# A hybrid decoder layer on one core: the fourth unit's delta net inputs ahead of the third unit's q and k projections, with two more homes for two buffers

## The chip, the core and the metric

The kernel runs on one core of one Trainium2 chip. The core has five engines with queues of their own: PE (TensorE, matmuls), DVE (VectorE), ACT (ScalarE), POOL (GpSimd) and SP (SyncE, which here only issues DMAs; ACT issues some too). [...] The metric is the device time of one execution in microseconds (us).

## The reference

One layer on 2048 tokens of width 1024, all float32. A first norm and one input projection feed three mixers side by side; their outputs are joined, projected, added to x, and a SwiGLU network follows:

```python
h = rms_norm(x, norm1_g)
u_conv, u_qkv, u_z, u_ab, u_dq, u_dk, u_dv = split(h @ w_in)
y_conv = conformer_conv_mixer(u_conv, ...)          # 31 taps, layer norm, silu
y_gdn  = gated_deltanet_mixer(u_qkv, u_z, u_ab, ...)  # 4 heads of 64, chunks of 64 tokens
y_diff = differential_attention_mixer(u_dq, u_dk, u_dv, ...)
x = x + concat([y_conv, y_gdn, y_diff]) @ w_out
gate, up = split(rms_norm(x, norm2_g) @ w_ffn_in)
x = x + (silu(gate) * up) @ w_ffn_out
return rms_norm(x, final_norm_g)
```

The delta net works by chunks of 64 tokens. For each chunk a lower triangular matrix (here L) is built from k, the gates g and beta; its inverse (here X64) is applied; then a scan carries a 64x64 state per head from chunk to chunk:

```python
lower = where(strict, beta * (k @ k.T) * decay, 0)
sol   = triangular_solve(lower + eye, [v * beta, k * beta * exp(g)])
def step(state, inp):                  # 32 chunks, one after the other
    v_new = u_i - w_i @ state
    o_i   = (q_i * exp(g_i)) @ state + qk_i @ v_new
    state = state * exp(g_last) + (k_i * exp(g_last - g_i)).T @ v_new
```

## The kernel before

The 2048 tokens are four units of 512 (u = 0 to 3), each of four token tiles of 128. Products that need float32 accuracy are three matmuls of split operands (mm3, lines 137 to 139). The program text makes the mixers' part of the kernel as a list of steps, each a letter and a unit (line 937):

- N: ln1, the first norm of a unit; eight groups of four transposes (tiles ntp, line 292) that ACT and DVE write as the two halves of h (tiles ht, lines 302 and 303).
- I: gdn_in, inputs of the delta net: z and the gates (PSUM tiles mz, one per token tile), then q, k, v in six tiles (mq) with their short convolution (gdn_conv), and between them gdn_decays, which makes L and QKT.
- G: gdn_unit: k k^T and q k^T (tiles kk), products into L and QKT; the 32x32 inverses on DVE in 31 steps (tm, Tt, lines 470 and 472), out to DRAM and back as the merged inverse X64 (tile X in the trace), whose last block needs yp and wp; then the scan over eight chunks (tiles vp, op, dp, state Sbd).
- C and L: the convolution mixer: projections mg and mv and 62 tap instructions on DVE (tiles cp, ca); then its layer norm (tiles ctp, ctq).
- K and V: q, k projections (eight tiles ma, each with a second half ql on DVE) and v projections (mw), stored to DRAM.
- A: attention of the first unit (tiles s, pt, po, to).

After the list come the first half of unit 0's output projection (tiles hp, fed by hx), and the rest: attention of units 1 to 3 mixed with output projection (po from line 137) and the SwiGLU network (pg, pu, pd) of unit after unit.

The framework writes every engine's queue when the program is built, by readiness on its own estimate and by priority: an instruction's place in the text, moved ahead where the text says hp(n). So the list of steps is an order of preference and no barrier. What is strict are the buffers. A tile belongs to a tag with a number of slots. Tags that matter here: wp (split weights, 3 slots, every weight piece of the kernel takes the next one); wraw (raw weights before their split, 2 slots of 1024 numbers per partition; the split of w_in is kept in DRAM after unit 0, so units 1 to 3 load wp directly and take no raw slot); mm0 and mm1 (two PSUM banks, in turn for every tile mz, mq, mg, mv, ma, mw and unit 3's ctp, ctq); tp (2 PSUM banks for ntp, kt1, gtp and others); L, dd and tg (one slot each in pool gd: L; the decays' tg and the merge's ys share dd; the decays' bm and the inverses' tm share tg); X64 is one constant tile for all units. Pools gd and ps_sc (two PSUM banks of the scan) end after hp, and the output projection's tiles take their place.

Of the kernel before, what the change touches and what calls it, by code (L numbers as in the profile page):

```python
# [10 lines left out]
F32 = mybir.dt.float32  # L11
# [7 lines left out]
P = 128  # L19
# [5 lines left out]
TU = U // P  # L25
IN_W = 3080
H = 4
C = 64
DFF = 2816
NF = DFF // P  # L30
WS = 1024
# [11 lines left out]
def bcast(ap, n):  # L43
    return ap.unsqueeze(len(ap.shape)).to_broadcast(list(ap.shape) + [n])
# [3 lines left out]
def body(ctx: ExitStack, tc: tile.TileContext, x, norm1_g, w_in, conv_dw_w, conv_dw_b,  # L48
# [3 lines left out]
    V, G, A, T = nc.vector, nc.gpsimd, nc.scalar, nc.tensor  # L52
# [20 lines left out]
    def cst(shape, name):  # L73
        return const.tile(shape, F32, name=name, tag=name)
# [23 lines left out]
    wpool = ctx.enter_context(tc.tile_pool(name="wpool", bufs=1))  # L98
    wcount = [0]

    def hp(n=4000):
        return tc.high_priority(offset=n)
# [57 lines left out]
    def bank(*b):  # L160
        return Rot([P, 512], F32, *b)
# [14 lines left out]
    gd = gctx.enter_context(tc.tile_pool(name="gd", bufs=1, side="right"))  # L176
# [34 lines left out]
    nc.sync.dma_start(stg[33:34, 0:256], conv_ln_b)  # L211
    stq = gd.tile([4, 768], F32, name="stq", tag="L")
    nc.sync.dma_start(stq, gdn_conv_w[0])
# [31 lines left out]
    V.memset(ones, 1.0)  # L245
    Sbd = cst([P, 2, P], "Sbd")
    V.memset(Sbd, 0.0)
    X64 = cst([P, H, TU, C], "X64")
    V.memset(X64, 0.0)
    hist4 = cst([P, 6, 3], "hist4")  # L250
    V.memset(hist4, 0.0)
    hist30 = cst([P, 2, 30], "hist30")
# [127 lines left out]

    def gdn_decays(u, sc):

        L = sc["L"] = gd.tile([P, H, TU, C], F32, name=f"L{u}", tag="L")
        QKT = sc["QKT"] = gd.tile([P, H, TU, C], F32, name=f"Q{u}", tag="QKT", bufs=2)

        def m4(m):
            return m.unsqueeze(1).unsqueeze(1).to_broadcast([P, 2, H, C])

        for t0 in range(0, TU, 2):
            t2 = slice(t0, t0 + 2)  # L390
            tg = gd.tile([P, 2, H, C], F32, name=f"tg{u}_{t0}", tag="dd")
            V.tensor_tensor(tg, m4(mT), bcast(sc["g"][:, t2, :], C), op=ALU.mult)
            gr = ps_ga.tile([P, 512], F32, name=f"gr{u}_{t0}", tag="ga")
            T.matmul(gr, lhsT=bones, rhs=tg.rearrange("p t h c -> p (t h c)"), start=True, stop=True)
            bm = gd.tile([P, 2, H, C], F32, name=f"bm{u}_{t0}", tag="tg")
            G.tensor_tensor(bm, m4(mN), bcast(sc["be"][:, t2, :], C), op=ALU.mult)
            Lt, Qt = (d_[:, :, t2, :].rearrange("p h t c -> p t h c") for d_ in (L, QKT))
            V.tensor_tensor(Qt, gr.rearrange("p (t h c) -> p t h c", t=2, h=H), bcast(sc["G"][:, t2, :], C),
                            op=ALU.subtract)
            V.tensor_tensor(Lt, Qt, m4(mN), op=ALU.mult)  # L400
            V.tensor_tensor(Qt, Qt, m4(mT), op=ALU.mult)
            A.activation(Lt, Lt, AF.Exp, scale=-1.0)
            A.activation(Qt, Qt, AF.Exp)
            G.tensor_tensor(Qt, Qt, m4(mT), op=ALU.mult)
            V.tensor_tensor(Lt, Lt, bm, op=ALU.mult)
# [22 lines left out]
        sc.update(c1=c1, c2=c2, c3=c3)  # L428

    def gdn_unit(u, qtok, sc):  # L430
        L, QKT = sc["L"], sc["QKT"]

        def qkh(tt):
            return qtok[:, tt, 0:512].rearrange("p (h d) -> p h d", d=C)
        for tt in range(TU):
# [10 lines left out]
            for hp in range(2):  # L446
                kk = ps_ga.tile([P, 512], F32, name=f"kk{u}_{tt}_{hp}", tag="ga")
                kv = kk[:, 0:256].rearrange("p (a b c) -> p a b c", a=2, b=2)
                for p in range(2):
                    for ch in range(2):  # L450
# [3 lines left out]
                                 skip_group_check=True)  # L454
                for d_, b in ((L, 0), (QKT, 1)):
                    V.tensor_tensor(d_[:, hp::2, tt, :], kv[:, :, b, :], d_[:, hp::2, tt, :], op=ALU.mult)
        nc.scalar.dma_start(gL[u].rearrange("h (t p) c -> p (h t) c", p=P), L.rearrange("p h t c -> p (h t) c"))

# [18 lines left out]
        for ch in range(2):  # L477
            for blk in range(2):
                r0 = ch * C + blk * 32
                nc.scalar.dma_start(  # L480
                    X64[r0:r0 + 32, :, :, blk * 32:blk * 32 + 32].rearrange("p h t c -> p (h t) c"),
                    gT[u][1, blk].rearrange("h (t c) s q -> c s (h t) q", c=2)[ch])
# [4 lines left out]
        for ch in range(2):  # L487
            r0 = ch * C
            for th in range(TU * H):
                T.matmul(yp[r0:r0 + 32, th * 32:th * 32 + 32], lhsT=L[r0 + 32:r0 + 64, th % H, th // H, 0:32],  # L490
                         rhs=X64[r0 + 32:r0 + 64, th % H, th // H, 32:64], start=th == 0, stop=th == TU * H - 1,
                         skip_group_check=True)
# [9 lines left out]
        for r0 in (0, 64):  # L502
            A.mul(X64[r0:r0 + 32, :, :, 32:64].rearrange("p h t x -> p t h x"),
                  wp[r0:r0 + 32, :].rearrange("p (t h x) -> p t h x", t=TU, h=H), -1.0)
# [13 lines left out]
        def scan_tr(tt, ch, pg_, WQ, ps):  # L518

            cs = slice(ch * C, ch * C + C)  # L520
            for h in range(H):
                T.matmul(ps[h % 2 * C:h % 2 * C + C, 256 + h // 2 * C:256 + h // 2 * C + C], lhsT=pg_[cs, 4 + h, :],
                         rhs=X64[cs, h, tt, :], start=True, stop=True, skip_group_check=True)
            T.transpose(ps[:, 384:512], pg_[:, 2 * ch:2 * ch + 2, :].rearrange("p h d -> p (h d)"), ident)
# [6 lines left out]
        for tt in range(TU):  # L531
            _, kdv, WQ, zr = nin
            op = ps_sc.tile([P, 512], F32, name=f"op{u}_{tt}", tag="o")
            for ch in range(2):
# [6 lines left out]
                for h in range(H):  # L541
                    T.matmul(vp[cs, h * C:h * C + C], lhsT=X64[cs, h, tt, :], rhs=kdv[cs, 4 + h, :],
                             start=h == 0, stop=False, skip_group_check=True)
# [15 lines left out]
                for h in range(H):  # L559
                    p, hp = h // 2, h % 2  # L560
# [89 lines left out]
    def gdn_in(u):  # L650

        hts = HT[u]
        pc = w_in_pieces(COL_Z, 264)
        abt = gd.tile([P, TU, 8], F32, name=f"abt{u}", tag="abt")
        for tt in range(TU):
            ps = mmt(f"mz{u}_{tt}")
            y_tile(ps[:, 0:264], hts, pc, tt)
            zs = gd.tile([P, 256], F32, name=f"zs{u}_{tt}", tag="zs", bufs=2)
            with hp():
                V.tensor_copy(abt[:, tt, :], ps[:, 256:264])  # L660
                A.activation(zs, ps[:, 0:256], AF.Tanh, scale=0.5)
                V.scalar_tensor_tensor(zs, zs, 1.0, ps[:, 0:256], op0=ALU.add, op1=ALU.mult)
            nc.scalar.dma_start(zd[u * U + tt * P:u * U + (tt + 1) * P, :], zs)
        with hp(6000):
            SC[u] = gdn_gates(u, abt)
        with hp(DP):
            gdn_decays(u, SC[u])
        qtok = QT[u] = gd.tile([P, TU, 768], F32, name=f"qtok{u}", tag="qtok", bufs=2)
        for ft in range(6):
            ps = mmt(f"mq{u}_{ft}")  # L670
            x_tile8(ps, hts, w_col_piece(w_in, COL_QKV + ft * P))
            with hp(CP):
                gdn_conv(u, ps, ft, qtok)
            if ft == 3:
                with hp(SP):
                    gdn_scales(u, qtok, SC[u])
# [257 lines left out]


    CV = {}
    for step in ("I0 C0 G0 V0 N1 K0 L0 I1 G1 N2 C1 L1 K1 V1 I2 G2 C2 N3 K2 I3 G3 L2 C3 V2 A0 K3 V3 L3").split():
        what, u = step[0], int(step[1])
        if what == "N":
            HT[u] = ln1(u)  # L940
        elif what == "I":
            gdn_in(u)
        elif what == "G":
            with hp(GP):
                gdn_unit(u, QT[u], SC[u])
        elif what == "K":
            attn_qk(u)
        elif what == "V":
            attn_v(u)
        elif what == "C":  # L950
            CV[u] = conv_taps(u, conv_in(u))
        elif what == "L":
            conv_ln(u, CV[u])
        else:
            p1bctx.close()
            ps0 = ctx.enter_context(tc.tile_pool(name="ps0", bufs=1, space=PSUM, reuse_waits="tile"))
            b0 = slots(ps0, "b0", 4)
            sct, ptt, tot, pot = (bank(b) for b in b0)
            E0, W0 = (p1b.tile([P, 4096], F32, name=f"arena{g}", tag=f"ht{g}") for g in range(2))
            X0, X1 = (p1b.tile([P, D], F32, name=f"arenx{g}", tag=f"x1{g}") for g in range(2))  # L960
            Ep, Wp = cut(E0, 1024, 4), cut(W0, 1024, 4)
            Eq = [e[:, 512:1024] for e in Ep]
            AT.update(e0=Views(F32, *(e[:, 0:512] for e in Ep)), dm=Views(F32, Eq[0]), ob=Views(F32, *cut(Eq[1], 256, 2)),
                      e1=Views(F32, *Eq[2:4]), on=Views(F32, *(f3(c_) for c_ in cut(X0[:, 0:512], 256, 2))),
                      vv=Views(F32R, f4(Wp[0])), kk=Views(F32R, *cut(Wp[1], 512, 2)), pp=Views(F32R, f3(Wp[2])),
                      qq=Views(F32R, *(f3(c_) for c_ in cut(Wp[3], 512, 2) + cut(X1, 512, 2))))
            so_ = [0]

            def take(w, m):
                o = so_[0]  # L970
                so_[0] += w * m
                vs_ = cut(X0[:, 512 + o:], w, m)
                return Views(F32, *([v.rearrange("p (a b) -> p a b", a=2) for v in vs_] if w == 4 else vs_))
            AT.update(small(take))
            dm = dists(U)
            run(attn_unit(0))
# [287 lines left out]
```

## Time and profile before

| | before |
|---|---|
| runs, us | 2917.52, 2921.23, 2925.54 (median 2921.23) |
| the profiled execution: time, us | 2917.14 |
| its span from first to last instruction, us | 2915.4 |
| mean granted TensorE clock | 0.982 |
| PE busy | 2800.1 us (96%) |
| DVE, ACT, POOL busy | 1565.9, 1050.0, 1111.3 us |

Times inside the profile count from the first instruction. The four units' steps up to V3 fill the span to about 834 us; the stretch from there to about 992 us is the change of stage to the SwiGLU network, which fills the rest. The clock is granted as a share of full speed, 1.0 or 0.5. A line such as "idle before <- releaser" tells how long an engine stood before an instruction and what ended the wait. A busy PE isn't PE at its peak, since matmuls overlap: the distance from one start to the next is its real pace.

### The profile page before, as it was taken

The page shows a single profiled execution, that of the slowest core. Times are in us where ns is not written, and L with a number is a line of the kernel's source. Part 1 is how long each engine was busy: PE and PEld are TensorE (multiplying, and loading weights), DVE is VectorE, ACT ScalarE, POOL GpSimd, SP SyncE. Part 2 cuts the span into 40 slices and gives each one's busy share as a digit, 9 for nine tenths or more (in the row PEclk, how much of TensorE's full clock was granted, in tenths as well). Part 3 has the DMA queues.
Part 4 walks back from the last instruction along what each step waited for, and adds up shares of the span by engine and source line. Part 5 has one row for each costly group of instructions (what it writes and reads, how often), then busy time and mean ns, then how long its engine had stood idle before and what let it go on. Part 6 is the DMA issues. An engine that isn't in the chain of part 4 may idle for free.

```text
span 2915.4 us, 39754 instructions
## 1 busy us (share of the span) xinstructions
PE 2800.1 (96%) x14673; PEld 2284.4 (78%) x14673; DVE 1565.9 (54%) x3443; ACT 1050.0 (36%) x2237; POOL 1111.3 (38%) x1021
## 2 busy tenths in 40 slices
PE   7979989999988999999998999999999999999998
PEld 6867777778776788887877888887878888888886
DVE  8976776877766765565566655541332222422223
ACT  4333223322154544444455434442332222322222
POOL 4421010001033444344455434444644444444543
PEclk9989999999988999999999999999999999999999
DMA  7784573654776544444366344324343333323332
GB/s 253 242 274 153 178 232 127 207 179 138 254 200 219 144 131 122 112 126 118 108 182 203 86 130 120 93 88 151 102 149 99 96 94 101 116 87 102 101 94 87
DMA packets 404064, 422.52 MB, mean 145 GB/s; under 512 B 46448, under 2 KB 326170, under 8 KB 392606
## 3 DMA queue, kind: packets, MB, share of 16 engines
q1 hardware_dynamic: 344222, 373.31, 41.8%
q10 hardware_dynamic: 59648, 46.67, 5.1%
q8 instruction: 116, 1.90, 0.3%
q14 instruction: 78, 0.64, 0.1%
HBM read 344.35 MB, written 75.56 MB: 144 GB/s over the span
## 4 chain that ended last, share of the span: by engine, by line
PE 80%; DVE 8%; DMA 6%; issue 2%; ACT 2%; POOL 1%; ACTq 0%; SPq 0%; POOLq 0%; DVEq 0%
PE pg L137 6%; PE pg L138 6%; PE pg L139 6%; PE pu L139 5%; PE pu L137 5%; PE pu L138 5%; PE pd L137 5%; PE pd L138 5%; PE pd L139 5%; PE s L784 3%; PE pt L830 2%; PE po L137 1%; PE po L138 1%; PE po L139 1%; PE ma L137 1%
## 5 line engine op out<-in xcount | busy, mean ns | idle before, releaser
L121 POOL TENSOR_TENSOR wp<-wr,wp 128x512 fp32r<-128x512 f32 (+1 forms) x666 | 906.7, 1386 | 865.4 <-ACT wp L120 847.9
L120 ACT CAST wp<-wr 128x512 fp32r<-128x512 f32 (+1 forms) x666 | 378.6, 617 | 871.5 <-PE pd L139 229.1
L137 PE MATMUL pd<-wp,ac 128*128 128x512 f32 x704 | 279.8, 400 | 9.2 <-DVE x L1154 7.6
L1154 DVE TENSOR_TENSOR x<-x,pd 128x512 f32<-128x512 f32 x192 | 130.4, 685 | 285.6 <-PE pd L139 285.2
L137 PE MATMUL pg<-h,wp 128*128 128x512 f32 x704 | 279.6, 397 | 3.4 <-ACT h L1075 1.7
L138 PE MATMUL pd<-wp,ac 128*128 128x512 f32 x704 | 277.1, 394 | 2.1 <-POOL wp L121 2.1
L139 PE MATMUL pd<-wp,ac 128*128 128x512 f32 x704 | 277.5, 394 | 1.5 <-DVE ac L1138 1.5
L139 PE MATMUL pu<-h,wp 128*128 128x512 f32 x704 | 278.4, 396 | 0.0
L139 PE MATMUL pg<-h,wp 128*128 128x512 f32 x704 | 278.3, 395 | 0.0
L137 PE MATMUL pu<-h,wp 128*128 128x512 f32 x704 | 277.3, 394 | 0.6 <-DVE ft L1135 0.6
L138 PE MATMUL pu<-h,wp 128*128 128x512 f32 x704 | 277.8, 395 | 0.0
L138 PE MATMUL pg<-h,wp 128*128 128x512 f32 x704 | 277.6, 394 | 0.0
L1134 DVE SCALAR_TENSOR_TENSOR ft<-ft,pg 128x512 f32<-128x512 f32 x88 | 60.4, 686 | 244.1 <-ACT ft L1133 244.1
L784 PE MATMUL s<-kk,qq 128*128 128x512 f32 (+3 forms) x576 | 171.6, 384 | 5.5 <-DVE mx L787 5.1
L593 DVE SCALAR_TENSOR_TENSOR cp<-hc,cwT,cp 128x512 f32<-128x512 f32 x232 | 173.2, 747 | 2.5
L137 PEld LDWEIGHTS pd<-wp,ac 128*128 128x128 f32 x704 | 132.7, 188 | 45.8 <-DVE x L1154 15.1
L137 PEld LDWEIGHTS pg<-h,wp 128*128 128x128 f32 x704 | 132.3, 188 | 36.2 <-ACT wp L120 5.4
L139 PEld LDWEIGHTS pd<-wp,ac 128*128 128x128 f32 x704 | 132.5, 188 | 31.7 <-DVE ac L1138 3.1
L138 PEld LDWEIGHTS pd<-wp,ac 128*128 128x128 f32 x704 | 132.8, 189 | 30.2 <-POOL wp L121 3.5
L137 PEld LDWEIGHTS pu<-h,wp 128*128 128x128 f32 x704 | 132.3, 188 | 30.0 <-ACT wp L120 1.0
L138 PEld LDWEIGHTS pu<-h,wp 128*128 128x128 f32 x704 | 132.3, 188 | 29.7
L138 PEld LDWEIGHTS pg<-h,wp 128*128 128x128 f32 x704 | 132.3, 188 | 28.8 <-DVE h L1076 0.2
(389 smaller groups left out, 5866.0 us busy)
## 6 DMA issues: line engine op xcount, KB each, us to landing
wr<-in_w_ffn_in_dram SPq DMA_DIRECT2D x176, 512.0 KB, 3.9
wp<-ws SPq DMA_DIRECT2D x66, 1024.0 KB, 5.8
wr<-in_w_ffn_out_dram SPq DMA_DIRECT2D x88, 512.0 KB, 3.5
ws<-wp SPq DMA_DIRECT2D x22, 1024.0 KB, 6.9
wr<-in_w_out_dram SPq DMA_DIRECT2D x44, 512.0 KB, 3.6
arena<-vs SPq DMA_DIRECT2D x80, 256.0 KB, 3.8
kk<-ks SPq DMA_DIRECT2D x64, 256.0 KB, 5.0
qq<-qs SPq DMA_DIRECT2D x96, 128.0 KB, 4.5
```

The source lines that it names most:

```text
L120: A.copy(w[:, 0, q], raw[:, q])
L121: G.tensor_tensor(w[:, 1, q], raw[:, q], w[:, 0, q].bitcast(F32), op=ALU.subtract)
L137: T.matmul(ps, lhsT=lh, rhs=rh, start=start, stop=False)
L138: T.matmul(ps, lhsT=lh, rhs=rl, start=False, stop=False)
L139: T.matmul(ps, lhsT=ll, rhs=rh, start=False, stop=stop)
L593: V.scalar_tensor_tensor(acc2[:, ct, :] if j == 30 else acc, hj, w, acc, op0=ALU.mult, op1=ALU.add)
L784: T.matmul(sp[:, 0:w], lhsT=qq[c][:, l, q0:q0 + P], rhs=kt_[x][c][:, k0:k0 + w], start=l == 0, stop=l == 1)
L830: T.transpose(pt[:, col:col + P], ptile[b][kt // 8][:, (kt % 8) * P:(kt % 8 + 1) * P], ident)
L1134: V.scalar_tensor_tensor(t_, t_, 1.0, pg, op0=ALU.add, op1=ALU.mult)
L1154: V.tensor_tensor(xs_, xs_, pd, op=ALU.add)
```

## The change

In the list of steps, K2 (q and k projections of unit 2) goes from ahead of I3 and G3 to behind them. L of units 1 and 3 is a tile of tag wraw in place of the one slot of tag L. X64 of unit 2 is a tile of tag wraw, cleared by POOL; units 0, 1 and 3 keep the constant tile. No arithmetic is added but for that clearing.

```diff
-    X64 = cst([P, H, TU, C], "X64")
-    V.memset(X64, 0.0)
+    X64_ = cst([P, H, TU, C], "X64")
+    V.memset(X64_, 0.0)
...
     def gdn_decays(u, sc):
 
-        L = sc["L"] = gd.tile([P, H, TU, C], F32, name=f"L{u}", tag="L")
+        if u % 2:
+            L = wpool.tile([P, WS], F32, name=f"L{u}", tag="wraw", bufs=2).rearrange("p (h t c) -> p h t c", h=H, t=TU)
+        else:
+            L = gd.tile([P, H, TU, C], F32, name=f"L{u}", tag="L")
+        sc["L"] = L
...
     def gdn_unit(u, qtok, sc):
-        L, QKT = sc["L"], sc["QKT"]
+        L, QKT, X64 = sc["L"], sc["QKT"], X64_
+        if u == 2:
+
+            X64 = wpool.tile([P, WS], F32, name="X64b", tag="wraw", bufs=2).rearrange("p (h t c) -> p h t c", h=H, t=TU)
+            G.memset(X64, 0.0)
...
-    for step in ("I0 C0 G0 V0 N1 K0 L0 I1 G1 N2 C1 L1 K1 V1 I2 G2 C2 N3 K2 I3 G3 L2 C3 V2 A0 K3 V3 L3").split():
+    for step in ("I0 C0 G0 V0 N1 K0 L0 I1 G1 N2 C1 L1 K1 V1 I2 G2 C2 N3 I3 G3 K2 L2 C3 V2 A0 K3 V3 L3").split():
```

## Rows read from the trace of the kernel before

**Rows 1.** The page's head and its part 1: the span, then busy time, share of the span and instructions of each engine.

```profile
span 2915.4 us, 39754 instructions
PE 2800.1 (96%) x14673; PEld 2284.4 (78%) x14673; DVE 1565.9 (54%) x3443; ACT 1050.0 (36%) x2237; POOL 1111.3 (38%) x1021
```

**Rows 2.** Busy time by windows: the stretch and its length in us, then busy us (and instructions) of PE, PEld, DVE, ACT and POOL, the granted clock, the DMA share and GB/s. The seven stretches follow the projections: K2 with N3; I3; C3 and V2; K3; V3; the change of stage; the first output projection and second norm.

```profile
516.60:588.70 72.10, 72.10 (x443) 56.06 (x442) 63.14 (x148) 23.52 (x63) 4.98 (x8) 1.00 0.71 204
588.70:649.70 61.00, 56.35 (x354) 46.55 (x353) 42.88 (x132) 14.63 (x34) 5.64 (x4) 0.94 0.55 183
649.70:727.60 77.90, 77.90 (x628) 63.67 (x627) 57.71 (x137) 21.24 (x44) 10.55 (x13) 1.00 0.42 136
727.60:787.40 59.80, 59.76 (x318) 45.22 (x317) 49.97 (x118) 9.50 (x20) 3.31 (x4) 1.00 0.79 264
787.40:834.00 46.60, 42.71 (x428) 39.70 (x426) 21.37 (x69) 19.90 (x51) 14.14 (x16) 0.93 0.70 204
834.00:933.00 99.00, 88.41 (x546) 69.09 (x545) 68.56 (x226) 42.33 (x128) 34.34 (x48) 0.87 0.72 200
933.00:992.00 59.00, 53.99 (x256) 42.15 (x254) 49.16 (x123) 37.62 (x85) 32.62 (x32) 0.90 0.70 202
```

**Rows 3.** The timeline of PE (start us, length us, engine, line, operation, tiles, form) where one kind of projection follows another: the first matmuls of unit 2's ma; the first of unit 3's mz; the first of unit 3's mq; the first and the last of unit 3's mw.

```profile
516.63 0.39 PE L137 MATMUL ma<-ht,wp 128*128 128x512 f32 x1
516.86 0.39 PE L138 MATMUL ma<-ht,wp 128*128 128x512 f32 x1
...
583.03 0.28 PE L137 MATMUL mz<-wp,ht 128*128 128x264 f32 x1
583.15 0.28 PE L138 MATMUL mz<-wp,ht 128*128 128x264 f32 x1
...
604.23 0.50 PE L137 MATMUL mq<-ht,wp 128*128 128x512 f32 x1
...
787.27 0.28 PE L137 MATMUL mw<-wp,ht 128*128 128x256 f32 x1
...
833.61 0.28 PE L139 MATMUL mw<-wp,ht 128*128 128x256 f32 x1
```

**Rows 4.** The timeline where the first norm of unit 3 is: the first transpose; the last of gdn_unit's copies of unit 2 that frees a bank of tag tp; the last write of unit 3's h on DVE.

```profile
527.02 0.33 PE L292 MATMUL ntp<-ident,x 128*128 128x128 f32 x1
534.25 0.59 ACT L445 COPY kq<-kt 128x512 f32<-128x512 f32 x1 [0.58 <-PE kk L452]
588.34 0.33 DVE L303 SCALAR_TENSOR_TENSOR ht<-ntp,g1T,ht 128x128 fp32r<-128x128 f32 x1
```

**Rows 5.** Groups of instructions (line, engine, operation, tiles, form, count; busy us, mean ns; idle us before): DVE from 516 to 590 us.

```profile
L593 DVE SCALAR_TENSOR_TENSOR cp<-hc,cwT,cp 128x512 f32<-128x512 f32 x47 | 35.1, 747 | 0.4
L303 DVE SCALAR_TENSOR_TENSOR ht<-ntp,g1T,ht 128x128 fp32r<-128x128 f32 x32 | 10.7, 343 | 1.7 <-ACT ht L302 1.6
L711 DVE SCALAR_TENSOR_TENSOR ql<-ma,qh 128x512 fp32r<-128x512 f32 x4 | 2.8, 689 | 1.1 <-ACT qh L710 1.1
L708 DVE TENSOR_TENSOR ql<-ma,qh 128x512 fp32r<-128x512 f32 x4 | 2.7, 684 | 1.0 <-ACT qh L707 1.0
```

**Rows 6.** The same groups on PE from 516 to 583 us, those beside the projections: the norm's transposes, kk, and dp of the scan (four to a chunk).

```profile
L292 PE MATMUL ntp<-ident,x 128*128 128x128 f32 x32 | 5.2, 279 | 0.0
L452 PE MATMUL kk<-kq 64*64 64x128 f32 x40 | 3.3, 282 | 0.0
L557 PE MATMUL dp<-vn,kd 64*128 64x128 f32 x12 | 2.1, 297 | 0.0
```

**Rows 7.** The busy time of tile ma alone in the stretch of K2 of unit 2 (PE, PEld, DVE, ACT, then clock, DMA share, GB/s).

```profile
516.60:583.00 66.40, 48.38 (x192) 34.70 (x191) 4.80 (x7) 4.13 (x7) 1.00 0.70 209
```

**Rows 8.** The timeline of SP and PE around slots: the first raw piece of w_out, ahead of time; the last use of L of unit 3 (line 490); the load of hx into the slot of tag L.

```profile
180.98 0.37 SPq L118 DMA_DIRECT2D wr<-in_w_out_dram  x1
...
804.10 1.19 PE L490 MATMUL yp<-X,L 32*32 32x32 f32 x32 [1.60 <-DMA X<-gT]
...
805.33 0.34 SPq L1016 DMA_DIRECT2D hx<-in_x_dram  x1
```

**Rows 9.** The timeline of DVE where unit 3's decays begin: the first tile of tag dd, and the first write of L.

```profile
653.83 0.69 DVE L392 TENSOR_TENSOR tg<-mT,sg 128x512 f32<-128x512 f32 x1 [1.11 <-PE wp L500]
...
661.05 0.68 DVE L400 TENSOR_TENSOR L<-Q,mN 128x512 f32<-128x512 f32 x1
```

**Rows 10.** The timeline of PE in the change of stage: the first scores of attention; the first yp of unit 3; dp of the last chunk of its scan; the last hp; the first matmuls of unit 0's output projection.

```profile
788.10 0.34 PE L784 MATMUL s<-arena 128*128 128x128 f32 x2
...
801.34 1.17 PE L490 MATMUL yp<-X,L 32*32 32x32 f32 x32 [0.77 <-DMA X<-gT]
...
914.67 0.60 PE L557 MATMUL dp<-vn,kd 64*128 64x128 f32 x3
...
918.83 0.40 PE L139 MATMUL hp<-wp,hy 128*128 128x512 f32 x1
...
933.82 0.80 PE L137 MATMUL po<-wp,yt 128*128 128x512 f32 x1 [0.34 <-ACT yt L1086]
934.42 0.63 PE L138 MATMUL po<-wp,yt 128*128 128x512 f32 x1
934.85 0.63 PE L137 MATMUL po<-wp,yt 128*128 128x512 f32 x1
```

## The prediction

> **What bounds the kernel now.** I read first the page's head: PE is busy 96% of the span and no other engine over 54% [rows 1], so time is lost only where PE waits, or where it works at the lower clock. The second view is the busy time by windows, cut where one projection follows another [rows 2]. The reader should see two kinds of stretch. From 516.6 to 787.4 us PE is full but for 4.65 us in I3 (61.00 less 56.35) and a granted clock of 0.94 there. From 787.4 to 992 PE stands idle 3.9, 10.6 and 5.0 us, at a clock of 0.93, 0.87 and 0.90: this change of stage is where a reordering can gain. In its middle part the idle 10.6 us and the 13% of 99 us that the clock withholds (12.9) make 23.5 us of slack.
>
> The third view is PE's timeline at the seams [rows 3]. The projections run strictly in the order of the text: all of unit 2's ma (from 516.63) lies before unit 3's mz (583.03) [rows 7], then comes mq (604.23), and so on to the last mw of unit 3 (833.61). Text order alone would only be a preference; two banks taken in turn and three weight slots make it a queue. That tags are given in text order can be seen on another tag: hx reads only x, could have been loaded at any time, and SP was ready to look ahead, for it fetched w_out at 180.98; yet hx took the slot of L only at 805.33, as the last yp of unit 3 ended (804.10 and 1.19) [rows 8], although unit 3's own L was first written at 661.05 [rows 9] and the slot stood empty before that.
>
> What ends the change of stage: the last chunk of the scan of unit 3 (914.67), the last hp (918.83) and the attention that starts at 788.10 come to an end close together, and the output projection follows at 933.82 [rows 10]. Three chains of dependent steps share engines there, and all three have to end.
>
> **The change, part by part.**
>
> *The two new homes of L and X64.* L of unit 3 wasn't waiting for its slot: the decays began with tag dd, released by the merge of unit 2 (653.83, ended by wp), and L was written after that, at 661.05 [rows 9]. dd and tg still have one slot each, so unit 3's decays still follow unit 2's merge. The new L is worth 0. The second X64 lets unit 3's inverse land while unit 2's scan still reads its own; in the trace unit 3's first yp waits for its X loads [rows 10], so today the tile is not late either, but it would be once G3 comes earlier. The clearing on POOL is one pass over a tile; POOL works 5.64 of 61 us in I3 [rows 2] and nothing of the path is queued behind it: 0. In the text L1, X64b and L3 come before w_out's raw pieces, so the fetch at 180.98 [rows 8] moves behind the release of X64b and L3, about 800 us at latest. Its first reader is hp, near the end of the stage: 0, or one landing if late.
>
> *K2 behind I3 and G3: what PE has to do meanwhile.* From 516.63 [rows 3] the next projection is mz of unit 3, and that needs the first norm of unit 3, whose last write starts at 588.34 [rows 4]. Today 192 matmuls of ma lie over this wait [rows 7], at 0.23 us from start to start (516.63 to 516.86) [rows 3]: 44.2 us. They can't be taken early any more: their banks and weight slots come after mq's. Left for PE from 516.6 to 583 is 66.4 less 44.2, that is 22.2 us.
>
> How soon can the norm be done? DVE is its engine: 63.1 of 72.1 us busy [rows 2]. It alternates with the taps, 35.1 us; the norm's own 32 writes take 10.7; the eight ql, 2.8 and 2.7 us, leave with K2 [rows 5]. The norm also waits for banks of tag tp that gdn_unit's copies free (until 534.25) [rows 4]; these follow kk matmuls that stand in PE's queue between ma's, and will come a little sooner. Lower end: each of the 32 writes followed by one tap, 0.343 and 0.747 us, makes 35 us, from a first transpose at 521 in place of 527.02, so 556. Upper end: 588, as now. I take 570, nearer to the lower end, for lack of ql and of a queue on PE. From 516.6 to 570 are 53.4 us; the other work fills 22.2; three of four token tiles of mz, 96 matmuls at 0.12 us (583.03 to 583.15) [rows 3], fill 8.6. **PE stands idle 22.6 us** (8.6 for 556, 40.6 for 588).
>
> [...] In I3 4.65 us idle went with 0.94 of the clock, a loss of 3.7 us [rows 2]. The work inside the idle stretch loses nothing by it, only mq's start does: +3 us (0 to 10). [...]
>
> Against this, the idle time and the clock of I3 today, 4.65 and 3.7 us [rows 2], partly go: behind mq, ma then lies ready under gdn_unit's round trip through DRAM. I take 5 of 8.3 (0 to 8). After I3 and K2 the projections run 22.6 + 3 - 5 = 20.6 us late.
>
> Also moved: the loads of mz's and mq's pieces go ahead of K2's eight on SP, long before they are read; K2's 16 stores on ACT come later, and attention of unit 0 doesn't read them. 0, as ACT is busy 23.5 of 72.1 us.
>
> *G3 earlier.* One chunk of the scan: the 22.2 us less 5.2 of transposes and 3.3 of kk is 13.7 for three chunks and a part of a fourth (12 dp) [rows 6], some 3.9 us each. Today seven of eight chunks of unit 3 lie behind the last mw (833.6). mq comes 32 us earlier (572 for 604.23), but unit 3's decays hang on unit 2's merge, so I let G3 gain 15 to 20 us; with the last mw 20.6 us later, about four more chunks come before it: **+15.6 us** for the projections, and 15.6 less behind them.
>
> *The change of stage.* From the last mw to po are 99 us now. It loses the four chunks (15.6). Of its slack of 23.5 us I give back 10 (0 to 23.5): with the scan out of the way the two other chains wait less for their turn, but each stays a chain of single buffers, and attention starts behind unit 3's ma as now. **-25.6 us.**
>
> *The sum.* +22.6 +3 -5 +15.6 -25.6 = **+10.6 us**. The rest of the kernel shifts. The profiled execution took 2917.14 us, 4.1 under the median of 2921.23; against it the sum gives 2927.7, against the median 2931.8. I say 2931.
>
> **The rivals.**
>
> *The gap is filled and the tail pays.* The norm is done by 556, and the scan of unit 1, no longer in line behind ma, runs in the gap. Then 8.6 us idle, no loss by the clock, 8 gained in I3, and the change of stage gives 23.5: 8.6 - 8 - 23.5 = -23; with part of it, -15. That is 2898 to 2906. For it: PE's queue is empty, so every wait of the norm shortens. Against: taps fill DVE in any case. It decides whether the norm ends before about 562.
>
> *Nothing is paid back.* The norm ends at 588 as now, 40.6 idle, and attention and hp, being latency chains, keep their 83 us: 40.6 + 3 - 5 = +39, 2960. For it: DVE is 88% busy in that stretch and its taps stand earlier in the text than the norm.
>
> [...]
>
> *It doesn't do what it says.* If slots went by readiness, ma could fill the gap as today and the order would stay: 2921. hx [rows 8] speaks against it.
>
> *w_out takes both raw slots at 181 us*, ahead of L of unit 1; the delta net would stand until hp's weights are split, over 100 us: above 3020. The same row of hx speaks against it.
>
> **How the numbers follow.** About 0.3% (8.8 us) is what a measurement of this kernel can tell from no change. The forecast, +10.6, has 0.41: slower 0.22, within 0.15, faster 0.04, by its own bounds. The gap filled: 0.25 (faster 0.20, within 0.05). Nothing paid back: 0.17, slower. The clock: 0.10 (slower 0.08, within 0.02). No effect: 0.05, within. The raw slots: 0.02, slower. Together faster 0.24, within 0.27, slower 0.49. The range leaves out the far ends of the first rival, of the second, and the last: 2898 to 2958. Where the forecast alone holds, 2917 to 2947.
>
> **What would show it.** In the profile after: mz of unit 3 starts before 583 and mq at about 572; PE's idle time between 516 and 572 is near 22 us with the clock under 1.0; ma of unit 2 lies between mq and mg; unit 3's first yp comes before 801, and its last dp well before the last hp; the last mw ends near 870 and po starts near 944. The prediction is wrong if ma fills the gap, if the norm's last write starts before 560, or if po starts before 925.

## The result, and the profile after

The changed kernel takes **2948.5 us** (median of four runs, 2942.0 to 2954.6) against 2922.4 for the kernel before on the same chip (2917.5 to 2925.5): ratio **1.0090, 95% interval 1.0068 to 1.0113**, some 26 us slower. The forecast was +10.6 (2931), and its range, 2898 to 2958, holds the result; the narrower range in which the forecast alone was to hold, 2917 to 2947, does not, by 1.5 us. The profiled execution took 2952.4 us, 3.9 above the median.

The head of the page after, to be read beside [rows 1]:

```profile
span 2950.7 us, 39779 instructions
PE 2818.9 (96%) x14673; PEld 2297.6 (78%) x14673; DVE 1555.6 (53%) x3443; ACT 1048.9 (36%) x2237; POOL 1110.6 (38%) x1022
```

The same matmuls, 18.8 us more busy time of PE, and 35.3 us more span: part of the loss is PE working slowly, part is PE standing. Busy time by windows shows where (columns as in [rows 2]: PE, PEld, DVE, ACT, POOL, clock, DMA share, GB/s; line numbers of the changed kernel are up to 8 higher than in the kernel before, so yp of L490 stands at L498). The stretches are the norm of unit 3 with mz, I3, K2 of unit 2, V3, from the last mw to the last hp, and from there to the first pg; the last line is a part of the first stretch.

```profile
516.60:574.30 57.70, 52.30 (x375) 40.23 (x374) 49.16 (x136) 21.13 (x62) 7.94 (x9) 0.85 0.28 80
574.30:620.40 46.10, 40.86 (x176) 32.43 (x176) 43.00 (x129) 8.49 (x20) 0.59 (x2) 0.93 0.53 182
620.40:684.00 63.60, 62.99 (x451) 48.92 (x450) 32.05 (x71) 18.42 (x33) 4.73 (x4) 1.00 0.65 207
...
806.80:853.40 46.60, 41.63 (x429) 38.58 (x427) 18.07 (x59) 18.35 (x46) 12.16 (x14) 0.96 0.75 222
853.40:940.00 86.60, 78.96 (x459) 60.26 (x457) 53.91 (x183) 36.27 (x112) 28.57 (x42) 0.82 0.71 189
940.00:1021.00 81.00, 65.24 (x310) 50.42 (x309) 54.12 (x145) 41.26 (x94) 38.58 (x39) 0.83 0.61 180
...
520.00:540.00 20.00, 19.65 (x124) 15.03 (x123) 14.34 (x37) 6.19 (x16) 2.05 (x2) 0.58 0.14 42
```

In the first stretch PE counts as busy for 52.30 of 57.70 us, but its 375 matmuls are the short ones: the stretch of K2 before, 72.10 us long, had 443, and the 192 longest of those, ma, aren't among the 375. Busy time hides the missing ma here: what is left are short matmuls at a clock of 0.85 (0.58 in the middle part).

The timeline of the kernel after (columns as in [rows 3]), at the seams:

```profile
527.57 0.59 PE L137 MATMUL mz<-wp,ht 128*128 128x264 f32 x1
...
574.32 0.55 PE L137 MATMUL mq<-ht,wp 128*128 128x512 f32 x1 [1.36 <-DVE cp L601]
...
576.20 0.33 DVE L303 SCALAR_TENSOR_TENSOR ht<-ntp,g1T,ht 128x128 fp32r<-128x128 f32 x1
...
620.36 0.48 PE L137 MATMUL ma<-ht,wp 128*128 128x512 f32 x1
...
642.23 0.69 DVE L396 TENSOR_TENSOR tg<-mT,sg 128x512 f32<-128x512 f32 x1 [4.96 <-PE wp L508]
...
683.95 0.39 PE L137 MATMUL mg<-ht,wp 128*128 128x512 f32 x1
...
821.94 0.75 PE L498 MATMUL yp<-X,L 32*32 32x32 f32 x19 [3.00 <-DMA X<-gT]
...
853.12 0.28 PE L139 MATMUL mw<-wp,ht 128*128 128x256 f32 x1
...
939.85 0.39 PE L139 MATMUL hp<-wp,hy 128*128 128x512 f32 x1
...
943.73 0.71 PE L565 MATMUL dp<-vn,kd 64*128 64x128 f32 x4
...
962.03 0.80 PE L137 MATMUL po<-wp,yt 128*128 128x512 f32 x1 [1.58 <-ACT yt L1094]
```

Against [rows 3, 4, 10]: mq of unit 3 comes 30 us earlier, the last mw 19.5 later, but **the first yp of unit 3 comes 20.6 us later (821.94 for 801.34), not earlier**, its scan's last chunk 29 later (943.73 for 914.67), the last hp 21 later, po 28 later.

To compare kernels without the busy time, the tables below use the amount of PE work done. Each of the 14673 matmuls has a weight (the lower quartile of the distance to the next start, among matmuls of its tile, in the trace before), and the delay is how much later than before the same sum of weights is reached. Each line is one profiled execution; "780" means the point that the kernel before reached at 780 us.

```
us late at          500    560    740    780   1000   1280   2840
the change          1.5   28.1   20.6   19.1   31.4   31.8   34.8
```

Three parts: the gap (the stretch from 516.60 to 574.30, where the ma are missing) costs 27 us; 9 come back by 780; the change of stage then costs 12 (and 3 more come behind it).

### The profile page after: what moved, and what is told of

It is laid out like the page before. It is cut to its first block, busy times and chain, and to the rows that moved or that the text cites. A ratio compares the mean times of both kernels' runs of the same rounds, so it can differ in the third digit from the quotient of the medians.

```text
span 2950.7 us, 39779 instructions
## 1 busy us (share of the span) xinstructions
PE 2818.9 (96%) x14673; PEld 2297.6 (78%) x14673; DVE 1555.6 (53%) x3443; ACT 1048.9 (36%) x2237; POOL 1110.6 (38%) x1022
## 4 chain that ended last, share of the span: by engine, by line
PE 80%; DVE 8%; DMA 6%; ACT 2%; issue 2%; POOL 1%; SPq 0%; ACTq 0%; POOLq 0%; DVEq 0%
PE pg L137 6%; PE pg L138 5%; PE pg L139 5%; PE pu L139 5%; PE pu L137 5%; PE pu L138 5%; PE pd L137 5%; PE pd L138 5%; PE pd L139 5%; PE s L792 3%; PE pt L838 2%; PE po L137 1%; PE po L138 1%; PE po L139 1%; PE ma L137 1%
```

## The experiments

Twelve kernels. They differ from the change in the order of steps or in the homes of L and X64; only no_taps3 leaves work out (29 of the 31 taps of unit 3's convolution, in both of its halves). The first table gives ratios over the kernel before, and, from each kernel's trace, the first yp of unit 3, the last mw, the last chunk of unit 3's scan, and the length of unit 3's inversion with the number of conv taps that VectorE runs inside it. The starts of yp and the ends of mw and of the scan are meant. "Old homes": L under its tag, one X64.

```
                      median   ratio (95% interval)     yp   mw   scan  inversion, taps
before                2919-22                          801  834   915    64 us, 32
the change            2948.5   1.0090 (1.0068-1.0113)  822  853   944    83 us, 48
order_only            2941.9   1.0075 (1.0054-1.0096)  813  850   936    80 us, 46
buffers_only          2932.0   1.0029 (1.0013-1.0044)  806  831   928    64 us, 32
l_only                2924.3   1.0005 (0.9989-1.0021)  796  825   910
x64_only              2925.3   1.0002 (0.9988-1.0015)  804  831   916
c3_before_k2          2921.7   1.0008 (0.9989-1.0027)  796  854   908    67 us, 32
v2_in_gap             2918.7   0.9990 (0.9976-1.0004)  814  817   915    75 us, 46
v2_gap_old_homes      2931.0   1.0030 (1.0017-1.0042)  824  819   934    77 us, 45
v2_gap_c3_old_homes   2925.1   1.0009 (0.9997-1.0021)  808  822   914    63 us, 32
n3_early              2936.4   1.0062 (1.0046-1.0077)  826  822   929    63 us, 32
n3_early_c3           2939.6   1.0072 (1.0050-1.0094)  841  818   943    63 us, 32
no_taps3 (less work)  2944.1   1.0079 (1.0055-1.0103)  787  884   913    46 us, 3
half_k2               2932.4   1.0048 (1.0029-1.0067)  807  833   919    64 us, 32
```

```
us late at            500    560    740    780   1000   1280   2840
order_only            0.5   21.4   18.1   17.1   15.1   14.8   18.6
buffers_only          1.7    2.4    3.6    3.9   18.3   17.5   21.5
l_only               -6.2   -5.5   -5.5   -5.1   -0.1   -0.4    2.7
x64_only             -2.6   -2.7   -0.6   -0.4    0.3   -0.3    2.5
c3_before_k2         -3.4   19.0   12.1   10.0   15.6   12.6    3.0
v2_in_gap             0.8    3.7   -3.8   -4.3    5.2    3.2    0.6
v2_gap_old_homes      2.2    4.9    4.6    4.1   11.0   10.7   12.6
v2_gap_c3_old_homes  -2.9   -0.2   -0.7   -1.0    5.1    4.8    3.8
n3_early             -0.1    8.5    2.6    8.4   20.9   20.7   22.7
n3_early_c3          -2.0    6.6    3.5    5.5   24.3   25.0   29.3
no_taps3             -2.5   24.1   22.1   28.9   32.0   33.6   32.4
half_k2              -3.4   -2.5    3.9    5.7   12.1   13.2   13.4
```

The profiled executions lie from 6 us under to 6 us over the medians of their kernels (order_only 6.3 under, the shortest of its six; buffers_only 5.8 over, the longest of its twelve), so a difference of some 10 us between two of these lines may be that of two executions and not of two kernels.

### The change in its two parts: order_only and buffers_only

```diff
# order_only: order of the change, homes as before
-        if u % 2:
-            L = wpool.tile([P, WS], F32, name=f"L{u}", tag="wraw", bufs=2).rearrange(...)
-        else:
-            L = gd.tile([P, H, TU, C], F32, name=f"L{u}", tag="L")
+        L = gd.tile([P, H, TU, C], F32, name=f"L{u}", tag="L")
...
-        if u == 2:
-            X64 = wpool.tile([P, WS], F32, name="X64b", tag="wraw", bufs=2).rearrange(...)
-            G.memset(X64, 0.0)
# buffers_only: homes of the change, order as before
-  ... C2 N3 I3 G3 K2 L2 C3 V2 A0 K3 V3 L3
+  ... C2 N3 K2 I3 G3 L2 C3 V2 A0 K3 V3 L3
```

> Only the new order; L keeps its tag and the merged inverses their one tile. The taps theory (the stage between the projections and the blocks ends with unit 3's delta net, and its inversion became slow because the 62 conv taps of unit 3 now lie on VectorE at the same time) and the gap theory (TensorE's stream of projections is 19.5 us late after the empty stretch ahead of mz of unit 3, and this is passed on to the end) both lay everything on the order: 2942 to 2954 us, as the change itself. If the new homes cost something, this runs under 2938; if they repay part of the loss, over 2958.

> Only the new homes of L and of the second tile of merged inverses; the order of the kernel before. Both theories: no difference, 2916 to 2928 us, because unit 3's decays still follow unit 2's merge through the single slots of dd and tg. A time outside of that means that the homes do something by themselves.

The order alone makes 22 us of the 26 (0.0075 of 2921), its median just under the band named, the homes alone 8.5, above theirs. The two stand side by side in the delays of their profiled executions as well: order_only is late by 560 and loses nothing in the change of stage, buffers_only loses little until 780 and 14 us there. With the 6 us by which these executions lie off their medians, the second of the two differences is weaker than it looks. That decays of unit 3 aren't released sooner by the new homes holds: in the trace of the change VectorE waits 4.96 us for unit 2's wp and then writes tg, as in [rows 9].

### The homes one by one: l_only and x64_only

```diff
# l_only: buffers_only without X64b;  x64_only: buffers_only with L under its tag
```

> The order of the kernel before; of the new homes only that of L (units 1 and 3 in a raw weight slot), the merged inverses in their one tile. The two homes together ran 1.0029 of the kernel before, about 8.5 us. Slot theory (the homes keep both raw slots until about 800 us, so the two pieces of w_out that were fetched at 181 and 194 us come after 795): one piece is still early and the price is half, 2922 to 2929 us. Order theory (the new tiles only re-deal the order of the engines' queues, whatever becomes of w_out): any time between 2915 and 2932, without relation to the number of early pieces.

> The order of the kernel before; of the new homes only the second tile of merged inverses for unit 2, L under its tag. Slot theory: one piece of w_out early, half the price, 2922 to 2929 us; if the raw slot that the tile holds until unit 2's scan ends at about 790 to 800 is the costly one, 2927 to 2934 here and 2918 to 2925 with L alone. Order theory: any time between 2915 and 2932.

Neither alone can be told from no change, and each lies in the bands of both theories. The fetch of w_out, at 180.98 in [rows 8], moves as the text order says; here it is in buffers_only:

```profile
795.42 0.38 SPq L118 DMA_DIRECT2D wr<-in_w_out_dram  x1
```

but that is not the price: two runs below, v2_in_gap (1.0030 with the old homes, 0.9990 with the new), show the same two homes 12 us faster. In v2_in_gap too the first piece comes late, at 798.6. So late pieces of w_out, the price by the slot theory, don't cost this in every order.

### Which loss ends last: c3_before_k2 and v2_in_gap

```diff
# c3_before_k2
-  ... C2 N3 I3 G3 K2 L2 C3 V2 A0 K3 V3 L3
+  ... C2 N3 I3 G3 L2 C3 K2 V2 A0 K3 V3 L3
# v2_in_gap
-  ... C2 N3 I3 G3 K2 L2 C3 V2 A0 K3 V3 L3
+  ... C2 N3 V2 I3 G3 K2 L2 C3 A0 K3 V3 L3
```

> The change, with L2 and C3 put ahead of K2, so that the taps of unit 3 get onto VectorE before its inversion begins. The empty stretch ahead of mz of unit 3 stays. Taps theory: taps run from about 640 to 720 us, the inversion of unit 3 takes 60 to 66 us in place of 81, its first yp comes at 795 to 806 in place of 822, and the time is 2920 to 2932 although the last mw stays near 853. Gap theory: the projections end as late as in the change, and the time stays at 2943 to 2954.

> The change, with V2 put ahead of I3, so that its 192 matmuls (35 us in the trace of the change) fill the empty stretch ahead of mz of unit 3. Gap theory: the last mw comes back to about 834 us and with it the time to 2918 to 2930. Taps theory: the last mw comes back too, but conv_in of unit 3 is no earlier than in the change, its taps still lie on the inversion, the first yp of unit 3 comes at 820 to 835, and the time stays at 2942 to 2956.

**Each of the two remedies gives back the whole loss, so neither theory is the whole cause by itself.** c3_before_k2 keeps the gap (19 us late at 560, last mw at 854) and brings the first yp to 796; it is still 13 us late at 1280 and makes that up in the blocks behind, which wasn't followed further. v2_in_gap fills the gap, the last mw comes to 817 and the first yp stays at 814. Its rows on PE: V2 of unit 2 runs straight into mz, where the change had nothing but short matmuls:

```profile
561.22 0.28 PE L139 MATMUL mw<-wp,ht 128*128 128x256 f32 x1
561.34 0.28 PE L137 MATMUL mz<-wp,ht 128*128 128x264 f32 x1
...
813.56 0.65 PE L498 MATMUL yp<-X,L 32*32 32x32 f32 x9 [3.52 <-DMA X<-gT]
...
816.18 0.41 PE L139 MATMUL mw<-wp,ht 128*128 128x256 f32 x1
```

Why the inversion of unit 3 is slow in the change is seen in VectorE's groups over it (columns as in [rows 5]), taken from the first tm to the last Tt. The change:

```profile
L601 DVE SCALAR_TENSOR_TENSOR cp<-hc,cwT,cp 128x512 f32<-128x512 f32 x46 | 34.2, 743 | 0.1
L480 DVE TENSOR_TENSOR Tt<-Tt,tm 64x31 f32<-64x31 f32 (+15 forms) x31 | 10.2, 330 | 0.2
L478 DVE TENSOR_TENSOR tm<-Lg,Tt 64x31 f32<-64x31 f32 (+15 forms) x31 | 10.2, 328 | 0.2
```

c3_before_k2:

```profile
L601 DVE SCALAR_TENSOR_TENSOR cp<-hc,cwT,cp 128x512 f32<-128x512 f32 x29 | 21.6, 744 | 0.1
L480 DVE TENSOR_TENSOR Tt<-Tt,tm 64x31 f32<-64x31 f32 (+15 forms) x31 | 10.3, 331 | 0.4
L478 DVE TENSOR_TENSOR tm<-Lg,Tt 64x31 f32<-64x31 f32 (+15 forms) x31 | 10.2, 330 | 0.6 <-DMA Lg<-gL 0.3
```

The 62 steps of the inversion take 20.4 and 20.5 us. 17 taps more of this form lie between them, 12.6 us, and eight more small operations of unit 2's scan, 2.6 us: together nearly the 15.6 us between 82.7 and 67.1. (The table's 48 and 32 take the first and last form of a tap with them.) Before the change, taps of unit 3 began at 670 us and half were done when the inversion began at 723; with K2 ahead of C3, mg and mv come 34 us later, taps begin at 703, and the inversion, at 718, meets 48 of 62. The kernel before has 32, as c3_before_k2.

### The homes and the taps with the gap filled: v2_gap_old_homes and v2_gap_c3_old_homes

```diff
# v2_gap_old_homes: v2_in_gap with the old homes
# v2_gap_c3_old_homes: the old homes and
+  ... C2 N3 V2 I3 G3 L2 C3 K2 A0 K3 V3 L3
```

> V2 in the gap as in the run before of that name, with L and the merged inverses in their old homes. If the price of the homes and the effect of the order add up: 2918.7 less 8.5, 2905 to 2914 us, under the kernel before. If the homes cost only where the stage between the projections and the blocks is late, which it isn't with V2 in the gap: 2915 to 2922.

> Old homes, V2 in the gap and L2 and C3 ahead of K2: the empty stretch is filled and the taps of unit 3 lie ahead of its inversion. Gap theory: nothing beyond V2 in the gap, within 4 us of the run with V2 in the gap and old homes. Taps theory: unit 3's first yp comes before 800 us, the last chunk of its scan before 905, and the time is 5 to 15 us under that run. Third way: taps then lie where PE needs VectorE for mq's convolution and the norm of unit 3, and it is slower than that run.

The first missed on the other side: old homes cost 12 us here, where they gained 8.5 in the old order. The second goes the way of the taps theory, at its small end: 45 taps become 32, the inversion 77 becomes 63 us, the first yp 824 becomes 808, the scan ends 20 us earlier, and the time falls by 5.9 us. But yp doesn't come before 800 nor the scan's end before 905, as that theory had it, and the intervals (1.0017 to 1.0042 and 0.9997 to 1.0021) leave room for the 4 us or less of the gap theory.

### Whose gap it is: n3_early and half_k2

```diff
# n3_early
-  ... I2 G2 C2 N3 I3 G3 K2 L2 C3 V2 A0 K3 V3 L3
+  ... I2 N3 G2 C2 I3 G3 K2 L2 C3 V2 A0 K3 V3 L3
# half_k2: q2 and k2 are attn_qk for q and for k alone
+  ... C2 N3 q2 I3 G3 k2 L2 C3 V2 A0 K3 V3 L3
```

> The change, with N3 moved ahead of G2 and C2: unit 3's first norm stands ahead of unit 2's taps and inversion in the text. If the empty stretch is the norm's (its writes taking turns with taps on VectorE), mz of unit 3 follows unit 2's mv at about 517 without a stop, the last mw comes back from 853 to 830 to 836 us, and the time to 2920 to 2932 (the conv taps of unit 3 come some 20 us earlier as well). If PE waits there for something else than the norm (the slots of unit 2's delta net inputs), mz stops as in the change and the time stays at 2942 to 2954.

> The change, with the q half of K2 (96 matmuls, 22 us) put back ahead of I3 and the k half left behind G3. Gap theory: 22 us of work fill most of the 27 us that PE loses there, the last mw comes to 832 to 838, and the time to 2920 to 2932. If half of the eight splits that return to VectorE make the norm late by as much, mz stops longer and the time stays over 2936.

The gap is the norm's: with N3 early, mz follows mv without a stop, and the last mw comes at 822, 12 us earlier than before the change. And yet the kernel is 18 us slower than before, a miss of the time I had given. The rows of n3_early:

```profile
513.56 0.39 PE L139 MATMUL mv<-ht,wp 128*128 128x512 f32 x1
513.79 0.28 PE L137 MATMUL mz<-wp,ht 128*128 128x264 f32 x1
...
541.12 0.65 PE L460 MATMUL kk<-kq 64*64 64x128 f32 x8
...
602.35 0.20 DVE L478 TENSOR_TENSOR tm<-Lg,Tt 64x31 f32<-64x31 f32 x1 [1.82 <-DMA Lg<-gL]
...
821.38 0.28 PE L139 MATMUL mw<-wp,ht 128*128 128x256 f32 x1
...
826.37 0.84 PE L498 MATMUL yp<-X,L 32*32 32x32 f32 x12 [4.14 <-DMA X<-gT]
```

and of the change, the same kk and the same first tm of unit 2:

```profile
505.79 0.65 PE L460 MATMUL kk<-kq 64*64 64x128 f32 x8
...
553.04 0.19 DVE L478 TENSOR_TENSOR tm<-Lg,Tt 64x31 f32<-64x31 f32 x1
```

Unit 2's delta net, now behind the norm in the text for VectorE and for the banks of tag tp, has its first kk 35 us and its first tm 49 us later, and unit 3's decays stand behind its merge. So here the projections are early and the delta net of unit 3 is late, and the kernel loses 18 us.

half_k2 fills the gap (no delay at 560), and yp, mw and the inversion are as before to 6 us. It still takes 14 us more (2932.4, 0.4 above the band of the gap theory), 6 of them lost by 780 and 6 in the change of stage. What makes these isn't settled.

### Both remedies, and the taps taken away: n3_early_c3 and no_taps3

```diff
# n3_early_c3
+  ... I2 N3 G2 C2 I3 G3 L2 C3 K2 V2 A0 K3 V3 L3
# no_taps3: the change, with
-            for j in range(31):
+            for j in (0, 30) if u == 3 else range(31):
```

> The change, with N3 ahead of G2 and C2, and L2 and C3 ahead of K2: both remedies at once, the stretch filled by an early norm and taps ahead of the inversion. If the two causes are separate parts of the loss and nothing else bounds, 2905 to 2916 us, under the kernel before. If the stage behind the projections has a floor of its own (attention of the first unit and the output projection), 2916 to 2926, about as each remedy alone.

> The change, but the convolution of unit 3 leaves out 29 of its 31 taps (58 passes of VectorE, 43 us); all else stays. The empty stretch and the projections stay 19.5 us late. If taps beside the inversion of unit 3 are what the last stage loses, that inversion takes 45 to 60 us in place of 81, the first yp comes at 785 to 802 in place of 822, and 10 to 16 us of the 26 go: 2930 to 2938. If the last stage loses them by the two new homes and the order of the queues, 2942 to 2952, although the inversion is as short.

Both missed. In n3_early_c3 the taps of unit 3 now meet unit 2's inversion: it takes 70 us in place of 45 in n3_early, and the first yp of unit 3 falls to 841, the latest of all, with 21 us lost although the last mw is at 818. In no_taps3 the inversion is down to 46 us and the first yp comes at 787, 35 us earlier than in the change, and the time hardly moves (1.0079 for 1.0090, the intervals overlap). Its rows on PE:

```profile
786.86 0.81 PE L498 MATMUL yp<-X,L 32*32 32x32 f32 x20
...
883.42 0.28 PE L139 MATMUL mw<-wp,ht 128*128 128x256 f32 x1
...
959.45 0.39 PE L139 MATMUL hp<-wp,hy 128*128 128x512 f32 x1
```

Scan and attention now share PE with projections that were late already, the last mw comes at 883 and the last hp at 959, 30 and 20 us later than in the change. The early delta net behind a late stream of projections gained nothing here. That the lateness moved from one to the other because both want PE is how I read these rows; no run shows it by itself.

## Why the prediction was right in sign and short in size

The sign came from the gap, which was foreseen in size as well. That the time lies in the range owes something to luck: two of the later steps were wrong, one of them cancels in the sum, and the range was as wide as its rivals made it. Of the signs named beforehand mz (527.57), mq and the place of ma came as said; PE's idle time in the gap (5.4 us by busy time, not 22), the first yp, the last dp ahead of the last hp (943.73 and 939.85), the last mw (853, not 870) and po (962, not 944) did not.

**The queue order** [rows 3, 8] was right: ma of unit 2 lies between mq (to 618) and mg (683.95), and w_out's fetch moved behind the releases of the raw slots.

**The gap**, +22.6 and +3 for the clock, less 5: the projections were to be 20.6 us late behind I3 and K2, and the change is 20.6 late at 740 and 19.1 at 780. The parts hold roughly: 26.6 us lost from 500 to 560 for 25.6, 9 regained by 780 for 5, the norm's last write at 576.20 for 570, mq at 574.32 for 572. (The 8.6 us in this sum are three tiles of mz, which are 72 matmuls; the 96 named beside them are all four.) That the norm is the cause is shown by n3_early, and that the gap can be filled by v2_in_gap and half_k2. The form was other than I had put it: PE counts as busy nearly throughout (52.30 of 57.70 us).

**The clock in the gap** was rated as small. The +3 us was my estimate, and no run shows this term by itself; what the runs showed in its place are two kernels with the same order and different clocks. In the change the 20 us from 520 were granted 0.58; order_only was granted 1.00 in the same 20 us, and 0.74 later in the same gap, from 560 to 580:

```profile
520.00:540.00 20.00, 19.00 (x175) 14.71 (x173) 17.65 (x50) 8.47 (x25) 2.61 (x3) 1.00 0.34 102
560.00:580.00 20.00, 14.49 (x56) 10.79 (x55) 16.41 (x46) 4.05 (x12) 2.06 (x2) 0.74 0.51 153
```

It is 21.4 us late at 560, the change 28.1; at 740 they are 18.1 and 20.6. So some 7 us may be the clock's at 560, and at most 3 of them are left at 740. How long PE was busy doesn't tell the two kernels apart from 520 to 540: PE counts as busy 19.65 us at 0.58 in the one and 19.00 us at 1.00 in the other.

**G3 earlier by 15 to 20 us: this step failed.** The decays came 11.6 us earlier (642.23 for 653.83), and the inversion 5; but it took 83 us for 64, and the first yp came 20.6 us later. I had moved VectorE's taps with the projections only as far as mz's norm was concerned, and not asked what they would meet after C3 had been put behind K2. The runs that move taps (c3_before_k2, and the pair with the gap filled) show it: 13 to 16 taps out of the inversion, 14 to 16 us off it, and yp 16 to 26 us earlier. So the four more chunks of the scan that were to come before the last mw, +15.6 us, stayed behind it: the first chunk's dp starts at 850.28, 2.8 us ahead of the last mw (in the kernel before, 1.0 us behind it), and the other seven chunks follow. This is why the last mw is 19.5 us late and not 36.

**The change of stage giving 10 us back: this term failed, and with it the size.** From 780 to 1000 the change loses 12 us in place of gaining 10. The 15.6 us that I moved from one side of the last mw to the other cancel in the sum, so that they are wrong doesn't show in it; the 10 us of slack that weren't there, the 12 lost and the 3 that come later are the 25 us between the forecast of +10.6 and this execution's +35; against the median, +26, it is some 9 us less. In none of the thirteen kernels does this stretch give back more than 2 us.

I had counted idle time and clock of that stage as slack to be had. The clock, which the runs were not made to test, goes with the loss. These are the stretches from 780 to 1000 us before, and between the same sums of weights in the change, order_only and buffers_only; the last two lines, of the change and of buffers_only, lie inside theirs:

```profile
780.00:1000.00 220.00, 200.34 (x1303) 162.88 (x1302) 151.63 (x452) 105.17 (x273) 83.37 (x101) 0.90 0.71 201
799.10:1031.40 232.30, 203.93 (x1276) 164.10 (x1275) 137.91 (x423) 101.99 (x266) 82.26 (x98) 0.87 0.67 190
797.10:1015.10 218.00, 194.48 (x1278) 157.48 (x1278) 134.96 (x415) 103.00 (x265) 79.44 (x100) 0.92 0.70 203
783.90:1018.30 234.40, 212.62 (x1324) 170.88 (x1323) 150.32 (x456) 104.83 (x273) 80.38 (x100) 0.85 0.68 193
...
868.00:899.00 31.00, 27.23 (x128) 20.61 (x127) 16.39 (x63) 12.00 (x39) 5.78 (x10) 0.50 0.66 152
837.00:878.00 41.00, 38.94 (x183) 29.29 (x183) 22.88 (x87) 15.13 (x49) 12.13 (x20) 0.50 0.74 186
```

Length times the share of the clock that wasn't granted is 22, 30, 17 and 35 us: 8 more than before, 5 less and 13 more, beside 12 lost, 2 gained and 14 lost. In the change PE stands 8.7 us longer and is busy 3.6 us longer; in buffers_only it stands 2.1 us longer and is busy 12.3 us longer, and 41 us of its stretch were granted 0.50 while PE counted as busy for 38.94. Over 191 executions of these kernels, each compared with others of its own kernel, 0.001 of the mean granted clock goes with 2.2 us; the means are 0.982 before and 0.976 in the change. Whether the clock makes the loss or the loss the clock isn't shown, since no run holds one and moves the other, and PE was granted less where it stood, too (busy 14.49 us of 20 at the 0.74 above).

**The new homes at nothing**: not so in each order, 8.5 us with the old one (buffers_only) and -12 with V2 in the gap. The pieces alone cost nothing that can be told from noise. The homes do change the order in which the queues of SP, VectorE and ScalarE take their instructions from about 180 us on; which instruction makes the difference isn't settled. Neither is how much of the 12 us in the change of stage is the homes', how much the late yp's and how much the clock's: order_only, with yp at 813, lost nothing there, but in its shortest execution.

**What the times go with**, then, are two streams that share PE: the projections and the delta net of unit 3. The runs with one of them 12 to 20 us late and the other early (c3_before_k2, v2_in_gap) are level with the kernel before; those with both late (the change, order_only) lose 22 to 26; a delta net late by 25 to 39 (n3_early, n3_early_c3) loses 18 to 21 although the projections are early. A fit by least squares, made after the fact over the kernels that do all the work, gives 0.67 us per us of the first yp and 0.45 per us of the last mw, with 4.3 us of scatter: for the change 0.67 x 20.6 + 0.45 x 19.5 + 3.4 (its constant) = 26. The mean granted clock alone, fitted in the same way, leaves 7 us. The fit describes these kernels, half_k2 by 7 us too low and the two remedies by 7 too high, and is no test of the cause. The rival "nothing is paid back" (2960) was nearer in its mechanism than my forecast, though its norm at 588 was wrong. To the clock in the gap, which had 0.10 among the chances, at most 7 us at 560 and 3 at 740 can be laid.

Nothing here beats the kernel before by a measurable amount; v2_in_gap, at 0.9990 (0.9976 to 1.0004), comes nearest.

## What to carry to other kernels

When a step moves in a text order, follow its neighbours that moved with it: here C3 wasn't touched, but its taps reached VectorE 33 us later and met unit 3's inversion, a chain of 62 dependent steps that each tap in between (743 ns) made longer. Idle time in a stage where several chains end together is not slack until an experiment has taken it (in n3_early, n3_early_c3 and no_taps3 one chain came early and another late). And where a tile's new home re-deals the queues, treat some 10 us of either sign as open, and measure it in the order that will be kept. Read the granted clock of a stage beside its busy time: in buffers_only, at 0.85 for 0.90, PE was busy 12 us longer for the same work, which no row of waits shows.

## What the runs showed of the hardware that was not expected

PE can fall behind and count as busy: 19.65 of 20 us in the change at 520 to 540, with 124 short matmuls at a clock of 0.58, and 19.00 with 175 at 1.00 in order_only. The weighted sum of matmuls, not busy time, showed the loss. The clock differed between two kernels with the same order in the same 20 us (0.58 and 1.00, these two), and it was 0.50 for 41 us in buffers_only (837 to 878) while PE counted as busy for 38.94 of them.
